# Where the low half of an operand split is made: 64 subtractions of a fused two-block kernel go from VectorE to GpSimd

## The chip, the cores and the metric

The program runs on one core of one Trainium2 chip. The metric is the device time of one execution, in microseconds (us). The profile and the trace come from one execution, taken by the hardware profiler. The engines are called as the profile calls them: PE is TensorE's matmul (PEld its weight load), DVE is VectorE, ACT is ScalarE, POOL is GpSimd, and SP issues most of the DMAs.

## The reference, cut to what matters

The program computes two blocks on 1024 tokens of width 1024 in fp32. The changed lines touch three places: the gated feed-forward part of the first block, the norm at its end with the scale and shift of the second block's first layer, and the norm after that layer with the scale and shift of the next.

```python
def first_block(...):
    ...
        h = h + merged @ w_out[l]
        z = rmsnorm(h, ffn_norm_g[l])
        u = causal_dwconv(z @ w_up[l], conv_w[l], conv_b[l])
        h = h + (jax.nn.silu(u[..., :D_FF]) * u[..., D_FF:]) @ w_down[l]
    return rmsnorm(h[:, N_META:], final_norm_g)
...
def second_block(...):
    for i in range(DEPTH_2):
        ...
        if i % 2 == 0:
            sh, sc, gt = _adaln(c, ab_w_mod[j], ab_b_mod[j])
            h = x * (1.0 + sc[:, None]) + sh[:, None]
            y = _ab_mixer(h, ...)
            ...
            x = _post_norm(x, y, gt[:, None], ab_ln_g[j], ab_ln_b[j])
        else:
            ...
            h = x * (1.0 + sc[:, None]) + sh[:, None]
            f_in, f_gate, cq, ckv, kr, d_gate = _split_cd(h @ cd_w_in[j])
```

`_post_norm` is a layer norm of `ALPHA * x + gate * y`.

## The kernel before, in words

**Matmuls by splits.** PE multiplies fp32 operands in a shorter format, fp32r. Every operand is therefore kept as two parts in a tile of shape `[128, 2, n]`: a high part, which is the fp32 value copied to fp32r by ACT (line 746), and a low part, which is the value less its high part (line 747, a subtraction on DVE). A product of two such operands takes three matmuls for each slice of 128 rows: high weight by high input, high weight by low input, low weight by high input, in this order (`mm3`, line 87 of the profile). `split_act` makes the two parts of an activation; `split_in` does the same for weights that a DMA has brought, with the copy in line 79 and the subtraction in line 80.

**Order.** The program is written in loops, and a scheduler lays every engine's instructions out in one fixed queue when the program is built. At run time each engine takes its queue in that order and waits at an instruction until its inputs are there. Tiles come from pools: a tile whose buffer still serves an earlier reader waits for that reader.

**Unit (lines 936 to 952).** The token axis is cut in four pieces of 258 or 256 columns. The product with `w_up` is done as a block product with seven multiplications instead of eight, so it needs seven inputs T[0] to T[6] for each pair of token pieces, made from eight tiles `z[0]` to `z[7]` (named h in the rows) by sums and differences. There are two pairs, units 0 and 1. `unit` makes the inputs for k = 0 to 3; `put(i, x)` splits x into T[i]. T[0] and T[1] are the pieces as they are and are made early. T[4] is a piece as it is, and T[2], T[3], T[5] and T[6] are differences and sums, made in place. Unit 0's inputs are made during the product with `w_out` (matmuls of line 87, whose results line 898 adds to the residual), unit 1's at the beginning of the product with `w_up` (matmuls of line 1012 in `ffn_up`).

**First norm (`x1_chunk`).** After the last matmuls of `ffn_down` (line 1066, results added by line 1068) the tokens are treated in three chunks of 384, 384 and 256 columns. Per chunk the squares (ACT, line 1115) are added up on DVE (line 1120) and summed over the partitions by a matmul (line 1123); then for each of eight tiles DVE scales by the norm (line 1136), ACT applies scale and shift (line 1140) into one of four buffers, and `split_act` makes `hx`, the input of the second block's first matmuls.

**Second norm (`done` and `emit`, with `ln_chunk`).** The layer norm after that layer goes by the same chunks. `ln_chunk` subtracts the mean on DVE (line 1196), squares on ACT (line 1198), adds the squares up on DVE (line 1204) and sums them by a matmul (line 1207); `emit` multiplies by the norm (DVE, line 1456), scales and shifts (ACT, line 1462) and splits into `hx2` (`hx<-sqt` in the rows). The results of the layer's own last matmuls are added by line 1472 in between.

**POOL** works little: it issues DMAs of an earlier stage (line 1347) and does some memsets and, in the attention at the end, every other addition of 1024 columns (lines 1734 and 1736, `sa`), beside DVE, which does the rest.

Of the kernel before, what the change touches and what calls it, by code (L numbers as in the profile page):

```python
# [8 lines left out]
F32 = mybir.dt.float32  # L9
# [3 lines left out]
ALU = mybir.AluOpType  # L13
# [28 lines left out]
class Build:  # L42
# [696 lines left out]
                pass  # L739


    def split_act(self, t, lo, hi, src, scale=None):
        nc = self.nc
        h = t[:, 0, lo:hi]
        if scale is None:
            nc.scalar.copy(h, src)  # L746
            nc.vector.tensor_tensor(out=t[:, 1, lo:hi], in0=src, in1=h.bitcast(F32), op=ALU.subtract)
        else:
            nc.scalar.mul(h, src, scale)
            nc.vector.scalar_tensor_tensor(out=t[:, 1, lo:hi], in0=src, scalar=scale, in1=h.bitcast(F32), op0=ALU.mult, op1=ALU.subtract)  # L750
# [184 lines left out]
    def unit(self, z, T, n, ch):  # L935
        v = self.nc.vector
        (l1, h1), (l2, h2) = ch
        for k in range(4):
            a, b = z[k][:, l1:h1], z[k][:, l2:h2]
            c, d = z[4 + k][:, l1:h1], z[4 + k][:, l2:h2]  # L940
            put = lambda i, x: self.split_act(T[i], n * k, n * k + n, x)
            put(0, a)
            put(1, c)
            v.tensor_tensor(out=a, in0=a, in1=b, op=ALU.subtract)
            put(3, a)
            v.tensor_tensor(out=b, in0=d, in1=b, op=ALU.subtract)
            put(4, d)
            v.scalar_tensor_tensor(out=d, in0=a, scalar=-1.0, in1=d, op0=ALU.mult, op1=ALU.subtract)
            put(2, d)
            put(5, b)  # L950
            v.tensor_tensor(out=c, in0=c, in1=d, op=ALU.add)
            put(6, c)
            yield
# [173 lines left out]
    def x1_chunk(self, tp, c, lo, hi, rs):  # L1127
        nc, A = self.nc, self.A
        v = nc.vector
        if c == 0:  # L1130
            self.gf = self.load(self.const, "fin_g")
            self.hx = [self.actA.tile([128, 2, T1], F32R, tag="a", name=self.nm("hx")) for _ in range(8)]
        m = self.mod["ab"]
        for k in range(8):
            x = self.h1[k][:, 2 + lo:2 + hi]
            v.scalar_tensor_tensor(out=x, in0=x, scalar=self.gf[:, k:k + 1], in1=rs, op0=ALU.mult, op1=ALU.mult)
            if "x1" in self.dbg:
                nc.sync.dma_start(self.dbg["x1"][k][:, lo:hi], x)
            t = tp.tile([128, 384], F32, tag="tmp", name=self.nm("hx"), bufs=4)[:, 0:hi - lo]
            nc.scalar.activation(t, x, AF.Identity, scale=m[:, 8 + k, 0:1], bias=m[:, k, 0:1])  # L1140
            self.split_act(self.hx[k], lo, hi, t)


    def mods(self, pool, cp):
# [290 lines left out]
    def ab_x(self):  # L1435
        nc, A = self.nc, self.A
# [3 lines left out]
        with ExitStack() as es:  # L1440
# [8 lines left out]
            def done(c, lo, hi, ps):  # L1449
                n = hi - lo  # L1450
                if c == 0:
                    for k in range(8):
                        self.hx2.append(self.actA.tile([128, 2, T1], F32R, tag="a", name=self.nm("hx2")))

                def emit(k, d, rs):
                    v.tensor_tensor(out=d, in0=d, in1=rs, op=ALU.mult)
                    nc.sync.dma_start(self.resd[k][:, lo:hi], d)
                    t = sqt(k)[:, 0:n]
                    if c == 2 and k % 2:
                        v.tensor_scalar(out=t, in0=d, scalar1=sc[:, 0, k:k + 1], scalar2=sc[:, 1, k:k + 1], op0=ALU.mult, op1=ALU.add)  # L1460
                    else:
                        nc.scalar.activation(t, d, AF.Identity, scale=sc[:, 0, k:k + 1], bias=sc[:, 1, k:k + 1])
                    self.split_act(self.hx2[k], lo, hi, t)
                def sqt(k):
                    if k % 2 == 0:
                        self.sqp = tp.tile([128, 1024], F32, tag=("ap", "sg")[k // 2 % 2], name=self.nm("sqt"))
                    return self.sqp[:, 512 * (k % 2):512 * (k % 2) + 384]
                self.ln_chunk(tp, lambda k: self.rx(k, lo, hi), ps, n, emit, sqt, int(c == 2))
# [520 lines left out]
```

## Time and profile before

| what | value |
| --- | --- |
| three executions, median (lowest to highest) | 3126.2 us (3122.37 to 3130.72) |
| the profiled execution's own time | 3125.37 us |
| its span in the trace | 3123.5 us |
| granted PE clock, mean over the span | 0.987 of full speed |
| PE busy | 3000.8 us, 96% |
| DVE busy | 2023.9 us, 65% |
| ACT busy | 1177.7 us, 38% |
| POOL busy | 93.8 us, 3% |

The span is the part of the execution that the trace covers. The busy time of an engine is the time in which one of its instructions ran; an engine that isn't busy waits for another or has nothing to do. Where PE is busy without a break the stage lasts as long as its matmuls. The granted clock says which share of full speed the chip gave PE.

### The profile page before, as it was taken

What the parts mean: (1) busy time and instruction counts of PE and PEld (TensorE: products, weight loads), DVE (VectorE), ACT (ScalarE), POOL (GpSimd) and SP (SyncE); (2) the same over time, 40 slices, a digit from 0 to 9 for tenths busy, and PEclk for the clock granted to TensorE, in tenths of its full rate; (3) what the DMA queues carried; (4) which work ended last, traced back from release to release, by engine and by line L of the source; (5) the groups of instructions that cost most, each with busy time, mean ns of one, the idle gap of its engine ahead of it and who ended that gap; (6) DMA issues with size and microseconds to landing.
All of it is one profiled execution on the core that took longest, in us unless ns stands there. A gap on an engine that the chain in (4) does not pass through costs nothing.

```text
span 3123.5 us, 47333 instructions
## 1 busy us (share of the span) xinstructions
PE 3000.8 (96%) x19205; PEld 2667.8 (85%) x19205; DVE 2023.9 (65%) x3957; ACT 1177.7 (38%) x1851; POOL 93.8 (3%) x99
## 2 busy tenths in 40 slices
PE   8999989999999999989999999998999899999998
PEld 6999977878999999989999997897888787756567
DVE  6549567777456333588777767765434836588876
ACT  5342543332345321244333323234222526355553
POOL 0000000000120000000000000000000000022200
PEclk9999999999999999999999999999999899999999
DMA  4352454343463143432322355501111223400031
GB/s 152 93 167 89 135 193 139 111 137 109 146 183 108 61 133 111 142 95 101 109 100 104 102 183 202 175 29 36 55 48 43 94 70 102 137 4 8 26 110 55
DMA packets 125971, 327.76 MB, mean 105 GB/s; under 512 B 16974, under 2 KB 49966, under 8 KB 125558
## 3 DMA queue, kind: packets, MB, share of 16 engines
q1 hardware_dynamic: 119240, 304.12, 30.6%
q10 hardware_dynamic: 4464, 16.34, 1.3%
q0 software_dynamic: 2048, 4.26, 0.7%
q8 instruction: 151, 2.47, 0.3%
q14 instruction: 68, 0.56, 0.1%
HBM read 250.60 MB, written 73.39 MB: 104 GB/s over the span
## 4 chain that ended last, share of the span: by engine, by line
PE 83%; DVE 9%; ACT 4%; DMA 3%; issue 1%; SPq 0%; ACTq 0%; DVEq 0%
PE mm L87 46%; PE mm L1012 7%; PE sm L1012 7%; PE mm L1066 4%; PE sm L1066 4%; PE mm L1730 3%; PE mm L1284 2%; PE sm L1718 2%; PE sm L1694 1%; DMA YBd<-o 1%; DMA wm<-ab_w_mod 1%; ACT Tt L507 1%; PE sm L1167 1%; PE sm L470 1%; DVE R L609 1%
## 5 line engine op out<-in xcount | busy, mean ns | idle before, releaser
L87 PE MATMUL mm<-z,whl 128*128 128x256 f32 (+3 forms) x4032 | 682.2, 325 | 2.9 <-ACT whl L79 1.5
L87 PEld LDWEIGHTS mm<-z,whl 128*128 128x128 f32 x4032 | 638.5, 190 | 35.9 <-issue 27.4
L80 DVE TENSOR_TENSOR whl<-wraw,whl 128x1024 fp32r<-128x1024 f32 (+2 forms) x200 | 232.9, 1166 | 212.1 <-ACT whl L79 211.7
L87 PE MATMUL mm<-hx,whl 128*128 128x512 f32 (+2 forms) x1608 | 359.5, 381 | 5.6 <-ACT hx L746 4.7
L87 PEld LDWEIGHTS mm<-hx,whl 128*128 128x128 f32 x1608 | 291.3, 189 | 62.6 <-ACT hx L746 5.4
L79 ACT CAST whl<-wraw 128x1024 fp32r<-128x1024 f32 (+2 forms) x200 | 200.2, 1003 | 219.9 <-PE mm L87 135.7
L1012 PE MATMUL sm<-a,whl 128*128 128x256 f32 x1584 | 214.9, 284 | 2.9 <-ACT a L746 1.7
L1012 PE MATMUL mm<-b,whl 128*128 128x258 f32 x1584 | 212.7, 284 | 0.0
L1012 PEld LDWEIGHTS sm<-a,whl 128*128 128x128 f32 x1584 | 201.1, 190 | 5.2 <-ACT a L746 2.4
L1012 PEld LDWEIGHTS mm<-b,whl 128*128 128x128 f32 x1584 | 199.8, 190 | 0.0
L87 PE MATMUL mm<-a,whl 128*128 128x258 f32 (+3 forms) x1344 | 185.2, 300 | 3.7 <-DVE whl L80 3.1
L87 PEld LDWEIGHTS mm<-a,whl 128*128 128x128 f32 x1344 | 184.0, 190 | 4.3 <-DVE whl L80 3.3
L87 PE MATMUL mm<-b,whl 128*128 128x384 f32 (+1 forms) x1152 | 181.6, 319 | 0.0
L87 PEld LDWEIGHTS mm<-b,whl 128*128 128x128 f32 x1152 | 181.4, 188 | 0.0
L87 PE MATMUL mm<-y,whl 128*128 128x256 f32 (+2 forms) x687 | 126.0, 342 | 5.9 <-DVE h L1472 4.1
L87 PEld LDWEIGHTS mm<-y,whl 128*128 128x128 f32 x687 | 110.4, 192 | 20.0 <-DVE h L1472 4.9
L1066 PE MATMUL mm<-g,g 128*128 128x512 f32 (+2 forms) x504 | 116.8, 377 | 4.0 <-ACT g L746 3.9
L1730 PE MATMUL mm<-m,KB 97*128 97x512 f32 x420 | 116.9, 398 | 1.3 <-ACT P L1731 1.3
L1066 PE MATMUL sm<-g,g 128*128 128x512 f32 (+2 forms) x504 | 116.9, 379 | 0.0
L1731 ACT ACTIVATE P<-mm 128x512 f32<-128x512 f32 x160 | 91.6, 596 | 66.0 <-PE mm L1730 48.3
L1695 DVE TENSOR_REDUCE mx<-sm 128x1 f32<-128x512 f32 (+1 forms) x192 | 103.8, 594 | 14.9 <-PE sm L1694 14.1
L1066 PEld LDWEIGHTS mm<-g,g 128*128 128x128 f32 x504 | 91.3, 190 | 21.7 <-ACT g L746 4.8
(586 smaller groups left out, 4656.1 us busy)
## 6 DMA issues: line engine op xcount, KB each, us to landing
wraw<-w_up SPq DMA_DIRECT2D x44, 512.0 KB, 3.8
wraw<-w_h SPq DMA_DIRECT2D x32, 512.0 KB, 3.8
wraw<-ab_w SPq DMA_DIRECT2D x32, 512.0 KB, 4.7
wm<-ab_w_mod SPq DMA_DIRECT2D x24, 512.0 KB
wm<-cd_w_mod SPq DMA_DIRECT2D x24, 512.0 KB, 4.6
gd<-ag SPq DMA_DIRECT2D x22, 512.0 KB, 2.9
av<-gd SPq DMA_DIRECT2D x22, 512.0 KB, 4.7
wd<-w_down SPq DMA_DIRECT2D x22, 512.0 KB
```

The lines of the kernel that those rows point to most:

```text
L79: self.nc.scalar.copy(t[:, 0], raw)
L80: self.nc.vector.tensor_tensor(out=t[:, 1], in0=raw, in1=t[:, 0].bitcast(F32), op=ALU.subtract)
L87: nc.tensor.matmul(ps, W[:, wp, wofs + 128 * k:wofs + 128 * k + 128], X(xp, kofs + k, lo, hi), start=first and k == 0 and i == 0, stop=las ...
L470: nc.tensor.matmul(pw[64 * g2:64 * g2 + 64, NC5 * r:NC5 * r + NC5], Bm[:, q, r, 64 * g2:64 * g2 + 64], ut[:, 2 * q + g2, :], start=True, s ...
L507: (v.tensor_copy if i == 0 and r == g2 else nc.scalar.copy)(Tt.rearrange("p (q g) c -> p g q c", g=2)[R, g2], S[P, 0:NC5, r, 4 * i:4 * i + ...
L1012: nc.tensor.matmul(ps, w[:, wp, o + 128 * k:o + 128 * k + 128], T[i][:, xp, n * k:n * k + n], start=k == 0 and q == 0, stop=k == 3 and q == 2)
L1066: nc.tensor.matmul(ps, w[:, wp, 128 * o:128 * o + 128], g[:, xp, lo:hi], start=n_ == 0 and i == 0, stop=n_ == len(ws) - 1 and i == 2)
L1284: nc.tensor.matmul(ps, X(xp, k, 128 * t, 128 * t + 128), wv[k // 4][:, wp, 256 * (k % 4):256 * (k % 4) + 256], start=k == 0 and i == 0, st ...
L1695: v.tensor_reduce(out=mx[:, qt, j:j + 1], in_=ps, axis=mybir.AxisListType.X, op=ALU.max)
L1718: mm = nc.tensor.matmul(po[64 * c:64 * c + 64, :], vv(t)[:, 64 * h:64 * h + 64], P[t][:, c], start=t == 0, stop=t == KT - 1)
L1730: nc.tensor.matmul(ps, K[0:97, kp, 128 * t:128 * t + 128], Q[0:97, qp, 512 * c:512 * c + 512], start=i == 0, stop=i == 2)
L1731: E[t] = nc.scalar.activation(Pt[:, c], ps, AF.Exp, scale=scale)
```

## The change

`split_act` gets a further argument, the engine that makes the low part. Where it is given, the subtraction is issued on POOL (`nc.gpsimd`) instead of DVE; its operands and its result are the same. It is given for the inputs T[2], T[3], T[5] and T[6] of both units (32 subtractions of 256 or 258 columns), and for the first two chunks of `hx` and of `hx2` (16 each, of 384 columns). After the change every line number beyond 742 is higher by one.

```diff
-    def split_act(self, t, lo, hi, src, scale=None):
+
+    def split_act(self, t, lo, hi, src, scale=None, low=None):
         nc = self.nc
         h = t[:, 0, lo:hi]
         if scale is None:
             nc.scalar.copy(h, src)
-            nc.vector.tensor_tensor(out=t[:, 1, lo:hi], in0=src, in1=h.bitcast(F32), op=ALU.subtract)
+            (low or nc.vector).tensor_tensor(out=t[:, 1, lo:hi], in0=src, in1=h.bitcast(F32), op=ALU.subtract)
...
-            put = lambda i, x: self.split_act(T[i], n * k, n * k + n, x)
+            put = lambda i, x: self.split_act(T[i], n * k, n * k + n, x, low=self.nc.gpsimd if i in (2, 3, 5, 6) else None)
...
-            self.split_act(self.hx[k], lo, hi, t)
+            self.split_act(self.hx[k], lo, hi, t, low=nc.gpsimd if c < 2 else None)
...
-                    self.split_act(self.hx2[k], lo, hi, t)
+                    self.split_act(self.hx2[k], lo, hi, t, low=nc.gpsimd if c < 2 else None)
```

The scheduler lays the queues anew. DVE in unit 0, ahead of the weight split `whl_13308` (line 80) for which PE waits: b_13058, b_13059, b_13061 and b_13062 are T[2], T[3], T[5] and T[6], b_13060 is T[4], and the h tiles are the pieces z. Before:

```order
L898 SCALAR_TENSOR_TENSOR h_1472_12583<-mm_13147,h_1472_12583 128x256
L948 SCALAR_TENSOR_TENSOR h_1500_12851<-h_1472_12583,h_1500_12851 128x258
L747 TENSOR_TENSOR b_13061<-h_1472_12583,b_13061 128x258
L903 TENSOR_TENSOR sqacc<-sqacc,sqt_13174 128x256
L747 TENSOR_TENSOR b_13058<-h_1500_12851,b_13058 128x258
L951 TENSOR_TENSOR h_1500_12851<-h_1500_12851 128x258
L944 TENSOR_TENSOR h_1479_12650<-h_1479_12650 128x258
L747 TENSOR_TENSOR b_13060<-h_1509_12923,b_13060 128x258
L747 TENSOR_TENSOR b_13062<-h_1500_12851,b_13062 128x258
L747 TENSOR_TENSOR b_13059<-h_1479_12650,b_13059 128x258
L946 TENSOR_TENSOR h_1479_12650<-h_1509_12923,h_1479_12650 128x258
L80 TENSOR_TENSOR whl_13308<-wraw_13309,whl_13308 128x1024
```

And after, the same stretch of DVE's queue:

```order
L949 SCALAR_TENSOR_TENSOR h_1500_12851<-h_1472_12583,h_1500_12851 128x258
L945 TENSOR_TENSOR h_1479_12650<-h_1479_12650 128x258
L899 SCALAR_TENSOR_TENSOR h_1472_12583<-mm_13147,h_1472_12583 128x256
L952 TENSOR_TENSOR h_1500_12851<-h_1500_12851 128x258
L947 TENSOR_TENSOR h_1479_12650<-h_1509_12923,h_1479_12650 128x258
L748 TENSOR_TENSOR b_13060<-h_1509_12923,b_13060 128x258
L904 TENSOR_TENSOR sqacc<-sqacc,sqt_13174 128x256
L949 SCALAR_TENSOR_TENSOR h_1509_12923<-h_1479_12650,h_1509_12923 128x258
L80 TENSOR_TENSOR whl_13308<-wraw_13309,whl_13308 128x1024
```

Only the low parts of T[4] (and of T[0] and T[1], earlier) are left on DVE, the sums and differences follow each other directly, and the weight split comes eight rows earlier in the queue (17 rows instead of 25 lie between the unit's first difference, line 944, and it).

POOL's queue in unit 1 (a_13695, a_13696, a_13698 and a_13699 are its T[2], T[3], T[5] and T[6]), the last twelve of 16 rows, in the queue right behind the 16 of unit 0 and ahead of those of `hx`. Before the change POOL's queue has nothing here: the DMAs of line 1347 are followed by the memsets of the attention.

```order
L748 TENSOR_TENSOR a_13698<-h_1467_12520,a_13698 128x256
L748 TENSOR_TENSOR a_13699<-h_1493_12784,a_13699 128x256
L748 TENSOR_TENSOR a_13695<-h_1500_12851,a_13695 128x256
L748 TENSOR_TENSOR a_13698<-h_1472_12583,a_13698 128x256
L748 TENSOR_TENSOR a_13699<-h_1500_12851,a_13699 128x256
L748 TENSOR_TENSOR a_13698<-h_1479_12650,a_13698 128x256
L748 TENSOR_TENSOR a_13696<-h_1486_12717,a_13696 128x256
L748 TENSOR_TENSOR a_13695<-h_1509_12923,a_13695 128x256
L748 TENSOR_TENSOR a_13698<-h_1486_12717,a_13698 128x256
L748 TENSOR_TENSOR a_13699<-h_1509_12923,a_13699 128x256
L748 TENSOR_TENSOR a_13695<-h_1512_12955,a_13695 128x256
L748 TENSOR_TENSOR a_13699<-h_1512_12955,a_13699 128x256
```

All sixteen stand in one queue, and the last but one is T[2]'s for k = 3.

DVE in the second norm, from chunk 0's products with the norm (h tiles, line 1456) to the first additions of chunk 1's squares (line 1204). Before, from the fifth product on:

```order
L1456 TENSOR_TENSOR h_2146_18884<-h_2146_18884,rsy_23019 128x384
L747 TENSOR_TENSOR hx_2634_22980<-sqt_23028,hx_2634_22980 128x384
L747 TENSOR_TENSOR hx_2635_22981<-sqt_23028,hx_2635_22981 128x384
L1456 TENSOR_TENSOR h_2147_18886<-h_2147_18886,rsy_23019 128x384
L1456 TENSOR_TENSOR h_2148_18888<-h_2148_18888,rsy_23019 128x384
L1456 TENSOR_TENSOR h_2149_18890<-h_2149_18890,rsy_23019 128x384
L747 TENSOR_TENSOR hx_2636_22982<-sqt_23039,hx_2636_22982 128x384
L747 TENSOR_TENSOR hx_2637_22983<-sqt_23039,hx_2637_22983 128x384
L1192 TENSOR_SCALAR mu_23162<-sm_23160 128x384
L1472 SCALAR_TENSOR_TENSOR h_2144_18880<-mm_23244,mod_ab,h_2144_18880 128x256
L747 TENSOR_TENSOR hx_2638_22984<-sqt_23050,hx_2638_22984 128x384
L747 TENSOR_TENSOR hx_2639_22985<-sqt_23050,hx_2639_22985 128x384
```

And after, from the fifth product on:

```order
L1457 TENSOR_TENSOR h_2146_18884<-h_2146_18884,rsy_23019 128x384
L1457 TENSOR_TENSOR h_2147_18886<-h_2147_18886,rsy_23019 128x384
L1457 TENSOR_TENSOR h_2148_18888<-h_2148_18888,rsy_23019 128x384
L1457 TENSOR_TENSOR h_2149_18890<-h_2149_18890,rsy_23019 128x384
L1193 TENSOR_SCALAR mu_23162<-sm_23160 128x384
L1473 SCALAR_TENSOR_TENSOR h_2144_18880<-mm_23244,mod_ab,h_2144_18880 128x256
L1197 TENSOR_TENSOR h_2142_18876<-h_2142_18876,mu_23162 128x384
L1197 TENSOR_TENSOR h_2143_18878<-h_2143_18878,mu_23162 128x384
L1197 TENSOR_TENSOR h_2144_18880<-h_2144_18880,mu_23162 128x384
L1197 TENSOR_TENSOR h_2145_18882<-h_2145_18882,mu_23162 128x384
```

The eight low parts have left this queue, and chunk 1's differences from the mean (line 1196, now 1197) follow the products directly. The squares of chunk 1 (ACT) write buffers that chunk 0's `sqt` tiles used, and so wait for POOL's subtractions from these.

## Rows read from the trace of the kernel before

**Rows 1.** The page, part 1: busy us, share of span, instructions.

```profile
PE 3000.8 (96%) x19205; PEld 2667.8 (85%) x19205; DVE 2023.9 (65%) x3957; ACT 1177.7 (38%) x1851; POOL 93.8 (3%) x99
```

**Rows 2.** Busy time by window: window, its length, each engine's busy us, clock, DMA.

```profile
1340.00:1370.00 30.00, 24.57 (x188) 23.91 (x188) 28.91 (x75) 14.77 (x36) 0.00 (x0) 0.94 0.25 77
1400.00:1422.00 22.00, 17.59 (x103) 15.30 (x104) 20.05 (x55) 10.02 (x26) 0.00 (x0) 0.84 0.08 28
2109.00:2136.00 27.00, 18.84 (x93) 16.76 (x92) 18.52 (x43) 17.35 (x40) 0.00 (x0) 0.81 0.07 21
2446.00:2493.00 47.00, 32.78 (x172) 28.68 (x171) 43.95 (x101) 32.05 (x68) 0.00 (x0) 0.82 0.37 123
```

**Rows 3.** Timeline, unit 0: start, length, engine, line, operation [idle before <- releaser].

```profile
1350.68 0.76 DVE L944 TENSOR_TENSOR h<-h 128x258 f32<-128x258 f32 x2
...
1359.11 1.22 DVE L80 TENSOR_TENSOR whl<-wraw,whl 128x1024 fp32r<-128x1024 f32 x1
...
1360.38 4.36 PE L87 MATMUL mm<-a,whl 128*128 128x256 f32 x22 [3.12 <-DVE whl L80]
...
1365.33 4.89 PE L87 MATMUL mm<-a,whl 128*128 128x254 f32 x39 [0.59 <-DVE h L898]
```

**Rows 4.** Chain of waits, window 1400 to 1422: total us, times, longest.

```profile
PE sm L1012 <- ACT a L746: 1.7, 3, 0.6
...
PE sm L1012 <- DVE a L747: 1.2, 3, 0.5
```

**Rows 5.** Timeline, unit 1.

```profile
1396.86 2.79 DVE L747 TENSOR_TENSOR a<-h,a 128x256 fp32r<-128x256 f32 x8
...
1408.25 0.76 DVE L944 TENSOR_TENSOR h<-h 128x256 f32<-128x256 f32 x2
...
1420.25 0.43 DVE L747 TENSOR_TENSOR a<-h,a 128x256 fp32r<-128x256 f32 x1
```

**Rows 6.** Timeline, first norm, end of chunk 1.

```profile
2121.59 1.22 PE L1123 MATMUL sm<-cse,ones 128*128 128x256 f32 x2 [2.30 <-DVE cse L1120]
```

**Rows 7.** Timeline, second norm, chunks 0 and 1.

```profile
2462.61 1.62 PE L1207 MATMUL sm<-sqt,ones 128*128 128x384 f32 x2 [6.39 <-DVE sqt L1204]
...
2468.89 7.00 PE L87 MATMUL mm<-hx,whl 128*128 128x384 f32 x38
...
2472.22 1.03 DVE L747 TENSOR_TENSOR hx<-sqt,hx 128x384 fp32r<-128x384 f32 x2
...
2478.58 1.02 DVE L747 TENSOR_TENSOR hx<-sqt,hx 128x384 fp32r<-128x384 f32 x2
```

**Rows 8.** Line 747 by form: count, ns min/median/max, first and last start.

```profile
L747 DVE TENSOR_TENSOR hx<-hx,hx x24: 415/552/560, 2091.9 to 2136.5; 128x384 fp32r<-128x384 f32 x16, 128x256 fp32r<-128x256 f32 x8
```

**Rows 9.** POOL: the attention's additions by tile, and a memset by line.

```profile
L1736 POOL TENSOR_TENSOR sa<-sa,P x12: 2370/2382/2990, 2759.6 to 2948.7; 128x1024 f32<-128x1024 f32 x12
...
L1980 POOL MEMSET const-float32-0.0<- 128x1 f32 x1 | 0.1, 104 | 0.2 <-issue 0.2
```

**Rows 10.** Timeline, three places in the attention where POOL works.

```profile
2759.61 2.37 POOL L1736 TENSOR_TENSOR sa<-sa,P 128x1024 f32<-128x1024 f32 x1 [10.20 <-ACT P L1731]
2760.14 2.39 DVE L1685 TENSOR_TENSOR qt<-qt,qu 32x512 f32<-32x512 f32 x1
...
2788.03 3.47 POOL L1734 TENSOR_TENSOR sa<-P,P 128x1024 f32<-128x1024 f32 x1 [18.15 <-ACT P L1731]
2788.10 1.16 DVE L1734 TENSOR_TENSOR sa<-P,P 128x1024 f32<-128x1024 f32 x1
2789.18 2.87 DVE L1752 TENSOR_TENSOR gt<-gt,rz 128x512 f32<-128x512 f32 x1
...
2826.66 2.38 POOL L1734 TENSOR_TENSOR sa<-P,P 128x1024 f32<-128x1024 f32 x1 [14.23 <-ACT P L1731]
2827.64 0.35 DVE L1666 TENSOR_TENSOR kt<-kt,mm 64x256 f32<-64x256 f32 x1
```

**Rows 11.** Line 1685, all its instructions: ns min/median/max.

```profile
L1685 DVE TENSOR_TENSOR qt<-qt,qu x16: 675/683/2389, 2695.9 to 2943.9; 32x512 f32<-32x512 f32 x16
```

## The prediction

> **What bounds the kernel now.** I read the page's busy table first: TensorE is busy for 96% of the span, DVE for 65%, POOL for 3% [rows 1]. So a microsecond counts only where TensorE stands still, and DVE is not the bound over the whole. Next I cut the span at the places where the 64 moved subtractions lie, with the table of busy time by window [rows 2]. There the picture is another one: in the stretch that makes unit 0's inputs DVE works 28.9 of 30 us, in unit 1's 20.1 of 22, in the second chunk of the first norm 18.5 of 27, in the second norm 44.0 of 47, and TensorE leaves 4 to 14 us of each idle, at a granted clock of 0.81 to 0.94. These are the few places where DVE sets the pace. Then I read the timeline of each to see which DVE instruction releases TensorE:
>
> - Unit 0: TensorE stands 3.12 us until the weight split `whl` of line 80, which starts at 1359.11, and 22 matmuls later 0.59 us for line 898 [rows 3]. Line 80 stands in DVE's queue behind all of the unit's work.
> - Unit 1: from 1411 on the matmuls of `ffn_up` eat the products' inputs as fast as they are made; TensorE waits 1.7 us in all for high parts and 1.2 us for low parts [rows 4]; the low part that starts at 1420.25 is the last but one [rows 5].
> - First norm, chunk 1: TensorE waits 2.30 us for the sum of squares of chunk 2, whose six additions stand on DVE behind the last low parts of chunk 1 [rows 6].
> - Second norm: TensorE waits 6.39 us for the sum of squares of chunk 1, which stands on DVE behind all eight low parts of chunk 0; then it works on matmuls of `hx`, chunk 0 [rows 7].
>
> **What is moved.** 64 subtractions leave DVE for POOL: 32 of 256 or 258 columns (0.43 us each [rows 5]) and 32 of 384 columns (0.55 us each [rows 8]). One after the other they cost DVE less, since neighbours overlap: eight of 256 columns take 2.79 us, so 0.336 each (2.79 less the 0.08 by which the last overhangs, over 8) [rows 5]; two of 384 take 1.03, so 0.47 each [rows 7]. DVE is relieved of 32 x 0.336 + 32 x 0.47 = 25.8 us. The copies on ACT stay, the DMAs of SP too.
>
> **What one costs on POOL.** The trace has no subtraction of this size there. The nearest rows are the attention's additions of 1024 columns, 2.37 to 2.38 us where nothing disturbs them, and a memset of one column, 0.104 us [rows 9]. A straight line through the two gives 0.68 us for 256 columns and 0.96 for 384. Bounds: purely proportional, 0.59 and 0.89; with another 0.25 us for each instruction, which no row excludes, 0.93 and 1.21. I take the line. A move thus doubles the time of each subtraction, which would be no harm if POOL worked beside DVE.
>
> **Whether it works beside DVE.** The attention stage shows that it does not. At 2759.61 POOL starts an addition; the DVE addition of line 1685, both inputs in SBUF, comes at 2760.14 and takes 2.39 us instead of its usual 0.68: it ends 0.55 us after POOL is through [rows 10, 11]. The other way round, a POOL addition that comes at 2788.03, together with one of DVE at 2788.10, takes 3.47 us, and DVE's next (512 columns) takes 2.87: POOL waited for DVE, took its turn between two DVE instructions, and DVE waited for it whole. A DVE addition with one input in PSUM, at 2827.64, takes 0.35 us in the middle of a POOL addition and waits for nothing [rows 10]. So POOL and those DVE instructions that read two tensors in SBUF take turns, one whole instruction each. The Trainium skill says the same ("SBUF — State Buffer", section "Who interferes with whom"): a DVE instruction with two SBUF inputs contends with a POOL instruction that reads SBUF, because its second input comes through the read port that the two engines share. By that rule the sum comes out as by the rows, and the trace agrees with it, at 2.39 against 0.68 us. This counts against the change: around the moved subtractions nearly all of DVE's work reads two SBUF tensors (lines 80, 797, 912, 944 to 951, 1120, 1136, 1196, 1204, 1456, and the low parts that remain). Only lines 898, 1068, 1192, 1472 and the evacuations of `ffn_up` read PSUM. What was 0.336 or 0.47 us on DVE becomes 0.68 or 0.96 us of the same shared resource.
>
> **The sum, place by place.** I lay POOL's and DVE's instructions in their new order end to end and let only the PSUM readers run beside POOL. The same arithmetic has to give the times of before: in unit 0, 25 rows from 1350.68 to line 80 at 0.336 make 8.4 us, so 1359.08, and the row says 1359.11 [rows 3]; in unit 1, 34 rows and a weight split of half the width (half of line 80's 1.22) from 1408.25 make 12.0 us, so 1420.28, and the row says 1420.25 [rows 5].
>
> 1. Unit 0. Ahead of line 80 there are now 17 DVE rows (two of PSUM) and nine or ten POOL subtractions that are ready by then: 17 x 0.336 + 9.5 x 0.68 = 12.2 us, less 0.3 to 0.7 beside PSUM readers: 1362.4 instead of 1359.1, and TensorE begins some 3.4 us later. After that, ahead of line 898, come line 80 itself, six DVE rows and the other six POOL ones, 1.2 + 2.0 + 4.1 us: TensorE's next matmuls, at 1365.33 now, could begin at 1370.1, 4.8 later, of which 3.4 are counted. **+5** (3.5 with the lower POOL prices, or if line 898 delays nothing).
> 2. Unit 1. Eight of DVE's 28 low parts are made long before, 16 go. Of the 34 rows 20 stay; with the weight split and 14 POOL subtractions they stand ahead of the last but one: 6.7 + 0.6 + 9.5 = 16.8 us from 1408.25, so it starts at 1425.1 and ends at 1425.8, where it ends at 1420.7 now. TensorE has nothing but these products then. **+5** (4 to 5.5).
> 3. First norm. In chunk 0 DVE has no gap; its queue holds line 1068, which frees TensorE's PSUM, so the chunk's eight POOL instructions cost about 0.7 us at the sum of squares. In chunk 1 eight of 0.96 replace eight of 0.47, +3.9; DVE idles 8.5 us of that stretch [rows 2], and I let its gaps take up near half: sum of squares +2.1. **+2.8** (1.5 to 4).
> 4. Second norm. Chunk 0: +3.9 in the same way, and ACT's squares of chunk 1 use the buffers that POOL's last subtractions still read, two more turns of 0.96: the sum of squares comes some 6 us later (2468.6 against 2462.6). In chunk 1 the low parts run from 2472.2 to 2479.6; eight of 0.96 and the eleven or so DVE rows of 0.47 between them take 12.9 us, to 2485, and what is left of chunk 0's delay comes on top, so about 2487, and the squares of chunk 2 with them. But here TensorE has other work, matmuls of `hx` that need chunk 0 alone (38 of them take 7.0 us [rows 7]), and fills later waits with it. Of two delays of 6 to 7 us I count a quarter, what those matmuls don't fill. **+3** (1 to 6, the worst known term).
>
> Sum 5 + 5 + 2.8 + 3 = +15.8 on the profiled execution's 3125.4 us: **3141 us**. That execution lies 0.8 under the median of three (3126.2), so the two may be taken as one. Nothing else should move: in POOL's queue its other work stands ahead of and behind these places, and SP's order is as before.
>
> **The rivals.**
>
> - *Relief*: short instructions interleave after all, POOL really works beside DVE. The rows above, with 0.68-us victims, speak against it. It would bring: line 80 earlier by eight rows, 2.6 us; unit 1 bound by 15 POOL subtractions from 1409, 1419.4 instead of 1420.7, so 1.3; the first norm 0.5; the second 3 to 4 of its 6.39. Together -8: 3117. It decides if a DVE subtraction beside a POOL one keeps its 0.43 us.
> - *Small delay*: they take turns, but the matmuls in hand swallow the norms' delays and POOL costs the lower price: 3.5 + 4 + 1 = +8.5, 3134; hardly to be measured.
> - *Dearer*: each POOL instruction costs 0.25 us more. Behind some 15 in each unit that is 3.8 us twice, about 2 in each norm, so near +27: 3153. For it speaks that a short instruction shows a fixed cost that 1024 columns hide; against it, that the memset of one column, which also pays such a cost, takes 0.104 us [rows 9].
>
> The page "GPSIMD Engine Reference" of the Trainium skill (section 3.1, "Elementwise — side-by-side cycle accounting") has 4497 ns for 2048 columns; a line through that and the 2.38 us here gives, as an estimate, 0.79 and 1.05 us, and the sum would be near +20; no run here shows it.
>
> **How the numbers follow.** Chances: as summed 0.55 (its own range 3135 to 3147), small delay 0.24, dearer 0.12, relief 0.09. Faster or slower by 0.3% is 9.4 us, about what can be told from no change. Relief at -8 lies just inside, but may bring more than I count: 0.06 of its 0.09 as faster. Same: the small delay, the rest of relief, and the lower edge of the main case: 0.29. Slower 0.65. The range from 3122 to 3154 leaves out relief and the end of dearer.
>
> **What would show it.** In the changed profile: POOL L748 at 0.7 us (256 columns) and 1.0 (384) or longer where it waits its turn; DVE's subtractions and scalings beside it at 0.7 to 1.4 instead of 0.43; TensorE's wait for line 80 in unit 0 at 6 to 7 us instead of 3.12, its waits for low parts in unit 1 at 6 instead of 1.2 and now for POOL; the waits for sums of squares longer. It is wrong if DVE's neighbours keep their 0.43, or if POOL's durations are far from 0.68 and 0.96.

## The result and the profile after

| | median (lowest to highest), us | executions |
| --- | --- | --- |
| before | 3127.06 (3120.29 to 3130.72) | 6 |
| after | 3144.58 (3140.29 to 3150.31) | 6 |

The ratio is 1.006, 95% interval 1.0044 to 1.0075: the change makes the kernel 14 to 23 us slower. The profiled execution took 3144.98 us with a span of 3143.2 us, 19.7 us more than before, at a clock of 0.984.

On the page, part 1 answers to [rows 1]; below it are two rows of part 5.

```profile
PE 3009.4 (96%) x19205; PEld 2673.0 (85%) x19205; DVE 2015.5 (64%) x3893; ACT 1177.5 (37%) x1851; POOL 168.2 (5%) x163
...
L87 PE MATMUL mm<-hx,whl 128*128 128x512 f32 (+2 forms) x1608 | 366.2, 384 | 22.0 <-ACT fx L1542 7.6
...
L1013 PE MATMUL sm<-a,whl 128*128 128x256 f32 x1584 | 213.3, 284 | 7.8 <-POOL a L748 6.3
```

DVE has lost 64 instructions but only 8.4 us of busy time, where 25.8 us of work were taken from it; POOL has gained 74.4. An instruction that waits for its turn counts as busy, and that is where the rest of DVE's relief is: measured against the median of the same form before, DVE's rows at the changed places are 16.8 us longer in all. Of TensorE's new idle time two releasers stand out: POOL in the product with `w_up`, 6.3 us, and an evacuation on ACT, `fx` (its copy of a finished product `mm`), 7.6 us, which the prediction did not name.

POOL's subtractions by form: count, ns min/median/max, first and last start.

```profile
L748 POOL TENSOR_TENSOR b<-h,b x16: 641/843/1620, 1353.2 to 1368.4; 128x258 fp32r<-128x258 f32 x16
L748 POOL TENSOR_TENSOR a<-h,a x16: 715/728/5761, 1412.0 to 1428.2; 128x256 fp32r<-128x256 f32 x16
L748 POOL TENSOR_TENSOR hx<-hx,hx x16: 1017/1154/1346, 2096.9 to 2124.9; 128x384 fp32r<-128x384 f32 x16
L748 POOL TENSOR_TENSOR hx<-sqt,hx x16: 1003/1183/5082, 2454.5 to 2491.3; 128x384 fp32r<-128x384 f32 x16
```

Undisturbed, 256 columns take 0.72 us and 384 take 1.00; the maxima of 5.76 and 5.08 us are waits, not work.

To see where the time went, PE's matmuls were counted in order of their starts, and the span between the starts of the same two matmuls was taken in both traces. Over all the runs below the early stages vary by up to 8 us and the three places by up to 2 where nothing was changed in them, so only larger differences mean something. Units 0 and 1 are added, since the cut between them shifts.

```
matmuls, by number in PE's order      before   after
to 9000, early stages                 1301.2   +1.5
9000 to 9800, units 0 and 1            120.9   +3.9
9800 to 14300, ffn_up, ffn_down        654.2   -0.2
14300 to 14700, first norm              78.3   +0.3
14700 to 16150, second block's layer   277.5    0.0
16150 to 16400, second norm             60.8  +11.1
16400 to the end                       614.8   +2.9
```

The timeline after, at the four places (start, length, engine, line, operation [idle before <- releaser]); it answers to [rows 3], [rows 5], [rows 6] and [rows 7]. Here and below only the rows that the text uses are shown; others lie between them.

```profile
1352.21 0.76 DVE L945 TENSOR_TENSOR h<-h 128x258 f32<-128x258 f32 x2
...
1355.96 10.01 POOL L748 TENSOR_TENSOR b<-h,b 128x258 fp32r<-128x258 f32 x11 [1.25 <-ACT b L747]
1357.84 0.97 DVE L947 TENSOR_TENSOR h<-h,h 128x258 f32<-128x258 f32 x1
1358.74 0.95 DVE L748 TENSOR_TENSOR b<-h,b 128x258 fp32r<-128x258 f32 x1
1361.27 1.75 DVE L80 TENSOR_TENSOR whl<-wraw,whl 128x1024 fp32r<-128x1024 f32 x1
1363.07 11.15 PE L87 MATMUL mm<-a,whl 128*128 128x256 f32 x69 [4.30 <-DVE whl L80]
...
1411.10 0.75 DVE L945 TENSOR_TENSOR h<-h 128x256 f32<-128x256 f32 x2
1412.04 16.89 POOL L748 TENSOR_TENSOR a<-h,a 128x256 fp32r<-128x256 f32 x16 [42.97 <-ACT a L747]
1416.81 0.41 DVE L748 TENSOR_TENSOR a<-h,a 128x256 fp32r<-128x256 f32 x1
1417.85 0.58 PE L1013 MATMUL sm<-a,whl 128*128 128x256 f32 x1 [3.00 <-POOL a L748]
...
2110.18 0.91 PE L1124 MATMUL sm<-cse,ones 128*128 128x384 f32 x2 [1.13 <-DVE cse L1121]
...
2128.56 0.70 PE L1124 MATMUL sm<-cse,ones 128*128 128x256 f32 x2 [1.78 <-DVE cse L1121]
...
2474.69 8.78 PE L87 MATMUL mm<-hx,whl 128*128 128x384 f32 x47
...
2491.86 0.63 PE L820 MATMUL sm<-sqt,ones 128*32 128x256 f32 x4
...
2497.53 0.59 PE L815 MATMUL sm<-sqt,ones 128*128 128x256 f32 x2
2497.78 1.90 PE L87 MATMUL mm<-hx,whl 128*128 128x384 f32 x9
...
2506.72 0.47 ACT L1542 COPY fx<-mm 128x384 f32<-128x384 f32 x1
2507.24 7.95 PE L87 MATMUL mm<-hx,whl 128*128 128x384 f32 x30 [7.56 <-ACT fx L1542]
```

The end of the second norm before, in the same view; these rows the prediction did not use.

```profile
2479.04 2.90 PE L819 MATMUL sm<-sqt,ones 128*32 128x256 f32 x14 [3.15 <-ACT sqt L1198]
...
2483.38 0.60 PE L814 MATMUL sm<-sqt,ones 128*128 128x256 f32 x2
2483.63 8.75 PE L87 MATMUL mm<-hx,whl 128*128 128x384 f32 x48
...
2492.58 0.47 ACT L1541 COPY fx<-mm 128x384 f32<-128x384 f32 x1
...
2493.10 12.11 PE L87 MATMUL mm<-hx,whl 128*128 128x384 f32 x77 [0.73 <-ACT fx L1541]
```

This is the difference that matters most. Before, the sums of squares of chunk 2 (line 819, last sum line 814) stand in PE's queue ahead of 48 matmuls of `hx` (the third weight panel on chunk 0 and the first on chunk 1), whose inputs are ready. From the start of the last sum to ACT's evacuation `fx`, which comes in ACT's queue behind the scalings and copies of chunk 2 and starts at 2492.58, there are 9.2 us, and the 48 matmuls cover them: TensorE waits 0.73 us. After, the scheduler has set most of these 48 among and ahead of the sums. At the last sum (line 815, 2497.53) nine are left, 1.90 us; the way to `fx` is as long as before (2506.72, again 9.2 us after), and TensorE stands 7.56 us.

The chain of waits of after, in unit 1 (window 1398 to 1430) and in the second norm (2450 to 2512): total us, times, longest.

```profile
PE sm L1013 <- POOL a L748: 6.3, 6, 3.0
...
PE sm L909 <- DVE sqacc L904: 2.5, 1, 2.5
...
PE sm L1013 <- ACT a L747: 1.5, 1, 1.5
...
ACT sqt L1199 <- POOL hx L748: 8.6, 7, 1.6
...
PE mm L87 <- ACT fx L1542: 7.6, 1, 7.6
```

### The profile page after: what moved, and what is told of

Its sections match the earlier page's. It is cut to its first block, busy times and chain, and to the rows that moved or that the text cites. A ratio compares the mean times of both kernels' runs of the same rounds, so it can differ in the third digit from the quotient of the medians.

```text
span 3143.2 us, 47400 instructions
## 1 busy us (share of the span) xinstructions
PE 3009.4 (96%) x19205; PEld 2673.0 (85%) x19205; DVE 2015.5 (64%) x3893; ACT 1177.5 (37%) x1851; POOL 168.2 (5%) x163
## 4 chain that ended last, share of the span: by engine, by line
PE 81%; DVE 9%; ACT 4%; DMA 3%; issue 1%; POOL 1%; SPq 0%; ACTq 0%; DVEq 0%; POOLq 0%
PE mm L87 45%; PE mm L1013 7%; PE sm L1013 7%; PE sm L1067 4%; PE mm L1067 4%; PE mm L1731 3%; PE sm L1719 2%; PE mm L1285 2%; DMA YBd<-o 1%; PE sm L1695 1%; ACT Tt L507 1%; DVE R L609 1%; PE sm L470 1%; ACT whl L79 1%; DMA wm<-ab_w_mod 1%
## 5 line engine op out<-in xcount | busy, mean ns | idle before, releaser
L87 PE MATMUL mm<-hx,whl 128*128 128x512 f32 (+2 forms) x1608 | 366.2, 384 | 22.0 <-ACT fx L1542 7.6
```

Source lines behind the costliest of these rows:

```text
L87: nc.tensor.matmul(ps, W[:, wp, wofs + 128 * k:wofs + 128 * k + 128], X(xp, kofs + k, lo, hi), start=first and k == 0 and i == 0, stop=las ...
```

## The experiments

Diffs are against the changed kernel unless the text says before. "Stages" are the surplus over the kernel before in units 0 and 1 / first norm / second norm, by the count of matmuls above; after itself has +3.9 / +0.3 / +11.1.

### One part alone

Three kernels give POOL one place each: the units (e1), the first norm (e2), the second norm (e3). As an example e1:

```diff
-            self.split_act(self.hx[k], lo, hi, t, low=nc.gpsimd if c < 2 else None)
+            self.split_act(self.hx[k], lo, hi, t)
...
-                    self.split_act(self.hx2[k], lo, hi, t, low=nc.gpsimd if c < 2 else None)
+                    self.split_act(self.hx2[k], lo, hi, t)
```

> Only the 32 low parts of the units are made by POOL; both norms as before. By the terms of the prediction +10 us (3136): +5 in unit 0, +5 in unit 1. By the trace of the changed kernel, where TensorE is 1.2 us late at the weight split of unit 0 but waits no longer for line 898 (0.59 before), and 3.5 us later after unit 1, +4 us (3130): a POOL subtraction beside DVE costs turns in unit 0, but DVE has given up 8 of 25 rows in exchange. Rival: all of it is fluctuation of the earlier stages and the units cost nothing, within 1 us of before.

> Only the 16 low parts of the first norm's chunks 0 and 1 are made by POOL. By the prediction's term +2.8 us (3129). By the trace of the changed kernel, in which TensorE is 5.4 us behind ahead of this stage and 5.7 behind it, +0.3 to +1 us: the matmuls in hand cover chunk 0 and the gaps of DVE take up chunk 1.

> Only the 16 low parts of the second norm's chunks 0 and 1 are made by POOL. By the prediction's term +3 us (3129): matmuls of hx in hand fill most of the two delays. By the trace of the changed kernel +11 us (3137): POOL's first subtraction of chunk 0 and of chunk 1 waits 4 to 5 us behind DVE instructions that follow each other without a pause, ACT's squares wait for POOL, ACT's weight copy and evacuations stand behind these, and so TensorE runs out of matmuls all the same (waits of 6.4 and 7.6 us). If the second is right, e1, e2 and e3 add up to about the 17 us of the whole change, with e3 more than half.

| run | ratio to before (95%) | worked out, us | stages |
| --- | --- | --- | --- |
| e1, units | 1.0018 (1.0009 to 1.0027) | +5.6 | +3.8 / +0.3 / 0.0 |
| e2, first norm | 1.0007 (0.9999 to 1.0016) | +2.2 | +0.3 / +2.2 / -0.5 |
| e3, second norm | 1.0045 (1.0029 to 1.0061) | +14.0 | -0.1 / +1.7 / +12.0 |

The microseconds are the ratio less 1 by the 3120.15 us of before on that chip. Their sum, 21.8, agrees with the whole within its interval. The second norm, forecast at +3, makes up most of it; the units cost about half of the +10 forecast. The first norm's cost lies between nothing and 2 us: e3, which changes nothing there, shows +1.7 as well.

### Low parts left out

POOL's subtraction becomes a memset to zero. The kernel leaves out the low parts of those 64 operands, so its time is that of a kernel in which neither DVE nor POOL makes them.

```diff
-            (low or nc.vector).tensor_tensor(out=t[:, 1, lo:hi], in0=src, in1=h.bitcast(F32), op=ALU.subtract)
+            if low:
+                low.memset(t[:, 1, lo:hi].bitcast(F32), 0.0)
+            else:
+                nc.vector.tensor_tensor(out=t[:, 1, lo:hi], in0=src, in1=h.bitcast(F32), op=ALU.subtract)
```

> The 64 POOL instructions only write zeros (a memset of the low part) and read nothing; so the low parts of these inputs are left out of the products. DVE is relieved of the same 64 subtractions. If the loss comes from POOL's subtractions (their reads of SBUF, their length, their turns), this must be faster than before: by the relief worked out in the prediction -8 us (3118), with DVE's neighbours at 0.42 us. If the loss comes from what else the change does (the new order of the queues, waits on POOL as such), it stays slower than before, above +5.

It took 3108.1 us, ratio 0.9962 (0.9948 to 0.9975), -11.9 us; stages -11.3 / -0.9 / +2.1. By form and from the timeline:

```profile
L749 POOL MEMSET hx<- x32: 417/418/425, 2044.7 to 2385.0; 128x384 f32 x32
...
L749 POOL MEMSET b<- x16: 303/304/314, 1284.3 to 1288.2; 128x258 f32 x16
```

```profile
2465.09 1.92 PE L87 MATMUL mm<-hx,whl 128*128 128x384 f32 x9
...
2474.62 5.58 PE L87 MATMUL mm<-hx,whl 128*128 128x384 f32 x22 [7.61 <-ACT fx L1545]
```

The memsets need no input and ran far ahead of their places (unit 0's by 1288.2), so this run does not show a POOL instruction working beside DVE's chains. DVE's and ACT's orders are those of after, and PE's differs in six places. What it shows is the worth of the relief: the units do gain 11 us when nobody makes these low parts, and TensorE never waits for them. So the loss is not that DVE's relief is worthless there, nor the new order of DVE; it is what the subtractions cost on POOL. In the second norm, where DVE is relieved of 16 instructions and POOL disturbs nobody, the stage is not shorter than before: TensorE still stands 7.61 us for `fx`. But PE's order there is that of after, with nine matmuls left at the last sum, so this run does not say that the relief is worthless in the second norm; what it gains may be hidden by the order (e11 below, an order like it with all low parts made, has +5.1, which is 3.0 more).

### Two of four inputs

Only T[5] and T[6] of the units go to POOL, 16 subtractions; both norms stay on DVE.

```diff
-            put = lambda i, x: self.split_act(T[i], n * k, n * k + n, x, low=self.nc.gpsimd if i in (2, 3, 5, 6) else None)
+            put = lambda i, x: self.split_act(T[i], n * k, n * k + n, x, low=self.nc.gpsimd if i in (5, 6) else None)
```

> Only T[5] and T[6] of both units on POOL (16 subtractions), both norms as before. TensorE needs these two last in unit 1, so POOL may be late with them while DVE gets to T[2] and T[3] 2.7 us earlier (8 x 0.336). If POOL's turns (0.59 us each beside DVE) and its lateness are the whole price: unit 0 about +1, unit 1 -1 to -2.5, within 2 us of before. If any subtraction on POOL costs the same wherever it is needed: half of the +4 us that the trace of the changed kernel shows for both units.

3123.06 us, ratio 1.0007 (0.9994 to 1.002); units +2.0. No gain that the measurement can see, and no loss: half the subtractions, and about half the surplus of e1 in the units.

### Each subtraction twice

e1, with every subtraction of the units done twice on POOL.

```diff
             (low or nc.vector).tensor_tensor(out=t[:, 1, lo:hi], in0=src, in1=h.bitcast(F32), op=ALU.subtract)
+            if low:
+                low.tensor_tensor(out=t[:, 1, lo:hi], in0=src, in1=h.bitcast(F32), op=ALU.subtract)
```

> As e1 (the units alone on POOL), but each POOL subtraction is made twice. If the price is POOL's turns and its own length: ahead of unit 0's weight split some 9 more turns of 0.59 us, +5; unit 1 has 15 more of 0.68 us ahead of the low part that TensorE needs, +10; so some 15 us above e1, 3140. If POOL's work were hidden, the time of e1.

3142.91 us, ratio 1.0075 (1.0056 to 1.0093); units +20.2, so 16.4 above e1. In the chain of waits of unit 1 TensorE now stands for POOL alone:

```profile
PE sm L1015 <- POOL a L750: 13.9, 7, 3.8
```

Here, where there is nothing to relieve DVE of, the 32 added instructions cost 0.51 us of TensorE's time each.

### Own buffers for the second norm

In the second norm ACT's squares of the next chunk waited 8.6 us for buffers that POOL's subtractions still read. e6 gives four of the eight `sqt` tiles of `emit` in chunks 0 and 1 a buffer of their own; e7 does the same to the kernel before.

```diff
-                    t = sqt(k)[:, 0:n]
+                    if c < 2 and k == 0:
+                        self.tq = yp.tile([128, 2, 1024], F32R, tag="y", name=self.nm("tq")).rearrange("p a b -> p (a b)").bitcast(F32)
+                    t = self.tq[:, 512 * k - 2048:512 * k - 2048 + n] if c < 2 and k > 3 else sqt(k)[:, 0:n]
```

> The changed kernel, but in the second norm the last four of eight scaled tiles of chunks 0 and 1 lie in a buffer of their own, so that the first four of ACT's squares of the next chunk find free buffers and the others wait for POOL's first four subtractions instead of its last. If ACT's squares waiting for POOL (8.6 us in all in the changed kernel's second norm) are what makes this stage late, its surplus over before falls from 11 us to 4 to 7, and the time to about 3139 against 3144. If POOL's late low parts themselves are what TensorE waits for, the stage stays at +11.

> The kernel before with the same buffers as e6 and all low parts on DVE: a control. Nothing waited for these buffers for long there, so the time is that of before within 2 us; if it gets faster by more, the gain of e6 is not to be put down to POOL.

e6: 3140.6 us, ratio 1.0067 (1.0047 to 1.0087), second norm +11.2, as without the buffers. e7: 1.0003 (0.9992 to 1.0013). From e6's chain of waits, and its timeline:

```profile
ACT sqt L1199 <- POOL hx L748: 0.6, 1, 0.6
```

```profile
2487.98 6.46 PE L87 MATMUL mm<-hx,whl 128*128 128x384 f32 x27 [2.09 <-POOL hx L748]
2494.37 0.62 PE L820 MATMUL sm<-sqt,ones 128*32 128x256 f32 x4
...
2509.74 5.49 PE L87 MATMUL mm<-hx,whl 128*128 128x384 f32 x16 [7.55 <-ACT fx L1544]
```

The wait was taken away, 0.6 us of 8.6 are left, and nothing was won. The sums of squares now start at 2494.37 directly behind 27 matmuls of `hx` in PE's queue: the order hides the gain. So the theory that the buffers alone were the cause fell, and PE's order had to be tried.

### PE's order in the second norm

e9 is e6 with one more rule for the scheduler: the third panel of `hx`, chunk 0, may stand only behind the last sum of squares of chunk 2, as it does before. e10 is after with the same rule, without the buffers.

```diff
-                self.panels(((w, ev), self.kv_panel(tp, 0), self.gate_panel(tp, 0, "gx", 1)), X, 8, CHX)
+                self.panels(((w, ev), self.kv_panel(tp, 0), self.gate_panel(tp, 0, "gx", 1)), X, 8, CHX, after=self.tailmm)
```

Here `tailmm` is that last sum, and `after` adds the rule to the panel's first matmul. e11 goes the other way: the kernel before, all low parts on DVE, with the norm of chunk 2 laid out so that PE's sums stand among the panels much as in after. In the traces e10 differs from after, and e9 from e6, in PE's order alone (36 places); e11 differs from before in 29 places of PE's order and also in about a dozen rows each of DVE's and ACT's.

```diff
-                self.ln_chunk(tp, lambda k: self.rx(k, lo, hi), ps, n, emit, sqt, int(c == 2))
+                with (self.tc.high_priority() if c == 2 else ExitStack()):
+                    self.ln_chunk(tp, lambda k: self.rx(k, lo, hi), ps, n, emit, sqt, int(c == 2))
```

> e6 with one ordering added on TensorE: the third panel of hx matmuls (chunk 0) and the fourth (chunk 1) come behind the sums of squares of chunk 2, as in the kernel before; in e6 and in the changed kernel these sums are interleaved with the end of the two panels, whose matmuls wait for POOL's low parts of chunk 1. If this order is what holds the last chunk back, the sums follow ACT's squares directly (squares end at 2491.7 in e6, the last sum at 2500.0), the two panels cover the chain after it again (TensorE's wait of 7.6 us for the evacuation goes below 2), and the stage's surplus falls from 11 to about 5 us: 3135 against e6's 3141. If POOL's low parts as such set the end, nothing is gained: 3141.

> The changed kernel itself with the same ordering as e9 and its own buffers. ACT's squares of chunk 2 still wait for POOL here (the last ends at 2493.1, the last sum at 2497.5), so the order alone gives back only some 2 us of the stage's 11: about 3142. If order alone is the cause it gives back as much as e9, 6 us; if the buffers alone mattered, e6 would have shown it.

> The kernel before, all low parts on DVE, but the scheduler is made to lay the sums of squares of chunk 2 among the third and fourth panel, as in the changed kernel (the layer norm's last chunk has another priority). If the order as such costs, its second norm is 3 to 7 us longer and TensorE waits for the evacuation there as in the changed kernel: 3125 to 3129 against 3120. If it costs only together with POOL's late low parts, the time of before within 2 us.

| run | buffers | PE's order | low parts | ratio (95%) | second norm |
| --- | --- | --- | --- | --- | --- |
| e11 | old | like after | DVE | 1.0025 (1.0015 to 1.0035) | +5.1 |
| e10 | old | like before | POOL | 1.0047 (1.0033 to 1.0061) | +6.9 |
| e6 | own | like after | POOL | 1.0067 (1.0047 to 1.0087) | +11.2 |
| e9 | own | like before | POOL | 1.0042 (1.0029 to 1.0054) | +2.3 |

The timelines of e11, e10 and e9 at the last sum and the wait for `fx`:

```profile
2480.76 0.59 PE L814 MATMUL sm<-sqt,ones 128*128 128x256 f32 x2
2481.00 2.97 PE L87 MATMUL mm<-hx,whl 128*128 128x384 f32 x15
2490.41 9.92 PE L87 MATMUL mm<-hx,whl 128*128 128x384 f32 x45 [6.43 <-ACT fx L1542]
```

```profile
2482.38 1.37 PE L823 MATMUL sm<-sqt,ones 128*32 128x256 f32 x4 [3.79 <-ACT sqt L1202]
...
2490.89 9.21 PE L87 MATMUL mm<-hx,whl 128*128 128x384 f32 x48
2500.58 1.66 PE L87 MATMUL mm<-hx,whl 128*128 128x384 f32 x8 [0.47 <-ACT fx L1545]
```

```profile
2481.30 2.89 PE L823 MATMUL sm<-sqt,ones 128*32 128x256 f32 x14 [3.75 <-ACT sqt L1202]
...
2485.43 8.75 PE L87 MATMUL mm<-hx,whl 128*128 128x384 f32 x48
2494.90 7.26 PE L87 MATMUL mm<-hx,whl 128*128 128x384 f32 x40 [0.73 <-ACT fx L1547]
```

e11, without one instruction on POOL, costs 5.1 us in that stretch and 7.8 us (4.7 to 10.9) in the time: the wait for `fx` is back, 6.43 us. Since rows of DVE and ACT moved with it, this is not PE's order by itself; e10 and e9 show that. PE's order restored gives 4.2 of after's 11.1 back with the old buffers, and 8.9 of e6's 11.2 with the own buffers; the wait falls to 0.47 and 0.73. The buffers give 4.6 more once the order is right, and nothing while it is not. What both leave, 2.3, is more than the -0.5 to +0.2 of the kernels that change nothing in the second norm (e1, e2, e5, e8, e12); its cause stays open. All four kernels are still slower than before.

### Only what is ready early

Only T[0] and T[1] of unit 1, whose eight low parts DVE makes at 1396.86 [rows 5], go to POOL.

```diff
-            put = lambda i, x: self.split_act(T[i], n * k, n * k + n, x, low=self.nc.gpsimd if i in (2, 3, 5, 6) else None)
+            put = lambda i, x: self.split_act(T[i], n * k, n * k + n, x, low=self.nc.gpsimd if i < 2 and l1 else None)
```

(Both norms stay on DVE.)

> Only the first two inputs of the second unit (8 subtractions of 256 columns) go to POOL; their high parts are cast 4 us before DVE's splits of that unit begin, so POOL can be through before DVE's chain starts. Theory (POOL costs only where its subtractions meet DVE's unbroken chain): DVE loses 8 times 0.336, 2.7 us, ahead of the sums for which PE waits 4.0 us, so the stretch of the two units is 1 to 3 us shorter than in the kernel before, and the time lies within 0.1% of it. Rival (every low part given to POOL costs about 0.15 us net, as in the whole set): 0 to 3 us longer. The time alone can hardly tell these apart; PE's stretch of the second unit is read beside it.

3120.12 us, ratio 0.9999 (0.9988 to 1.0011); units +0.8, unit 1 +0.2. The time is within what the theory gave, but the 1 to 3 us are not there. From the timeline:

```profile
1392.34 7.14 POOL L748 TENSOR_TENSOR a<-h,a 128x256 fp32r<-128x256 f32 x8 [466.91 <-ACT a L747]
1395.38 1.26 DVE L982 TENSOR_TENSOR whl<-wsum,whl 128x1024 fp32r<-128x1024 f32 x1 [2.13 <-ACT whl L981]
1396.57 0.94 DVE L904 TENSOR_TENSOR sqacc<-sqacc,sqt 128x254 f32<-128x254 f32 x1
1397.57 0.74 PE L909 MATMUL sm<-sqacc,ones 128*128 128x254 f32 x2 [4.11 <-DVE sqacc L904]
```

DVE was freed of its 2.8 us and then stood 2.13 us for ACT's copy of a weight, and the sum for which TensorE waits took a turn behind POOL, 0.94 instead of 0.42 us. TensorE waits 4.11 us, before 4.00:

```profile
1401.49 1.22 PE L908 MATMUL sm<-sqacc,ones 128*128 128x254 f32 x2 [4.00 <-DVE sqacc L903]
```

Another engine was next in line, so the relief was worth nothing at this place.

## Why the prediction was right in its total and wrong in two terms

The forecast of 3141 and the finding that POOL and DVE share a resource held; of the rivals, *relief* (-8), *small delay* (+8.5) and *dearer* (+27) lie outside the measured 14 to 23 us. But two terms missed in opposite directions: 10 forecast for the units and 3.9 measured, 3 for the second norm and 11.1 measured. That the total is nearer than its parts is luck: 6.1 too much and 8.1 too little nearly cancel.

**POOL's price.** The straight line gave 0.68 and 0.96 us; undisturbed, the last three of unit 1 together last 2.11 us with 0.73 for the last one, so they start 0.69 us apart; those of 384 columns last 1.00 to 1.02 at least. Right; *dearer* is out.

```profile
1426.82 2.11 POOL L748 TENSOR_TENSOR a<-h,a 128x256 fp32r<-128x256 f32 x3
```

**Taking turns.** DVE's rows in unit 0 last 0.95 and 0.97 us instead of 0.43 [rows 5], as forecast: longer by 0.52 to 0.54, most of one turn of the other engine (0.69). In unit 1 it went otherwise, see below. The page "SBUF — State Buffer" of the Trainium skill (section "Who interferes with whom") has the same rule for two SBUF inputs against POOL's reads, and the rows of unit 0 agree.

**Unit 0, forecast +5.** The step that was mis-sized is the price of a pair. I added a DVE row and a POOL row, 0.336 + 0.68 = 1.02 us; in the alternating stretch the two DVE rows above start 0.90 us apart with one POOL row between them. Over the whole stretch a POOL row cost still less: from the unit's first difference (1352.21) to line 80 (1361.27) DVE's 17 rows take 9.1 us, forecast 11.7, before 8.4 for 25; with the 0.53 us by which line 80 itself is longer, the nine POOL rows that start ahead of it cost DVE 0.43 us each on top of its own 0.336 a row, where 0.68 were counted. Some DVE rows had no POOL row beside them (POOL stood 1.25 us for a copy of ACT). The wait for line 80 grew from 3.12 to 4.30, not to 6 or 7, and the 0.59 us for line 898 are gone: TensorE's waits there grew by 0.6 us.

**Unit 1, forecast +5.** The step on the path was right: from the start of the first difference (1411.10) to that of the last but one low part (1427.51, 0.69 before the last) there are 16.4 us, forecast 16.8, before 12.0. But it came about in another way than told: POOL at first did not take turns, it stood 5.76 us behind DVE's chain and then ran nearly alone. DVE's neighbours kept their 0.41 us there, which the prediction had named as a sign of being wrong; yet POOL's wait made the sum the same. TensorE's waits for high and low parts rose from 2.9 to 7.8 us [rows 4], nearly the 5 forecast; its wait for the sum of line 904 fell from 4.00 (line 903 before) to 2.5, which I had not counted, and that for the sum before it grew from 2.83 to 3.14. Both units together: 0.6 + 0.3 + 4.9 - 1.5 = 4.3 us, and the count of matmuls has 3.9; behind these waits the granted clock fell towards the lower of its two levels (1.2 GHz) in other places, to a mean of 0.57 from 1403 to 1405 before and of 0.59 from 1394 to 1397 after, so the two need not agree more closely.

**First norm, forecast +2.8.** Between nothing and 2 us. The wait for the sum of squares of chunk 2 was 2.30 [rows 6] and is 1.78; that for chunk 1's, which had none, is 1.13. The runs cannot place the cost closer.

**Second norm, forecast +3.** Here a step failed, not only a size: "here TensorE has other work, matmuls of `hx` that need chunk 0 alone [...], and fills later waits with it", so that I counted a quarter of the delays. This took PE's queue as unchanged. The scheduler lays every queue anew, and had put those matmuls ahead of the sums of chunk 2; they no longer stood where they cover the chain to `fx`. I had looked at the rows of DVE and POOL and not at PE's. By the count of matmuls TensorE has lost 1.9 us in this stretch up to matmul 16370, just ahead of the wait for `fx`, and 11.1 up to 16390, just behind it. The runs put 4.2 us on that order with the old buffers (e10 against after), 8.9 with the new (e9 against e6), and 4.6 on ACT's squares that wait for POOL's reads once the order is right (e9 against e10). The two hide each other: each remedy alone brought at most 4.2 us, both together 8.8. That ACT's squares use buffers POOL still reads had been named, at two turns of 0.96 us; the row says 8.6 us, in seven waits.

**What DVE's relief was worth.** I had taken the second norm as a place where DVE sets the pace, 44 of 47 us [rows 2], and gave *relief* 3 to 4 us there. e4 takes the work away entirely and is not shorter there, since `fx` is late as in after; as PE's order is that of after too, no run shows what the relief is worth in the second norm under the order of before. In the units it is worth 11.3 us with nobody making these low parts, where *relief*, with POOL making them, counted 3.9. But POOL's subtractions cost more than the relief brings, and no kernel that computes everything came out faster than before.

Still open: the 2.3 us that e9 leaves in the second norm; the 2.9 us of after in the last stretch, which in the kernels that leave the second norm alone is between -0.5 and +4.2; and the 5.5 us by which e9's time (+13.1, interval 9.0 to 16.9) exceeds its three stages (3.0 + 2.3 + 2.3), of which 2.8 lie in the last stretch.

## What to carry to other kernels

When an instruction goes to another engine and a scheduler lays the queues, compare the queue of the bound engine, not only those of the two engines named in the change: here 4.2 of the 11.1 us of the largest term came back when PE's matmuls alone were put back in place, and 8.9 of 11.2 where the buffers had been parted too. Before work is moved to a spare engine, ask whether the two share something; the price can then be as much as the slower engine's time on the same resource, and the busy table does not show it. When one wait is taken away and the time stays, try the next in line together with it before the first is called innocent.

## What the hardware showed that was not expected

The two engines do not always take turns. In unit 0 they alternate, one instruction each. In unit 1 POOL's first subtraction starts at 1412.04 and lasts 5.76 us, through some fifteen DVE instructions that follow each other without a gap and none of which is longer than before (0.41 us). It ends about 0.6 us after the last of them (1416.81 + 0.41).

```profile
1412.04 5.76 POOL L748 TENSOR_TENSOR a<-h,a 128x256 fp32r<-128x256 f32 x1 [42.97 <-ACT a L747]
```

In the second norm two take 4.99 and 5.08 us in the same way. So, as far as these three rows go, an unbroken chain of DVE instructions with two SBUF inputs can keep POOL out for the whole of it; that the chain is the cause is read from the times and was not tried by a run. The section of the Trainium skill named above says that the issue order decides who blocks; by that one would expect POOL's instruction to go ahead of the later of those fifteen, and these rows differ. In unit 0 POOL did get in between neighbouring DVE instructions (0.97 and 0.95 us above), and in the first norm none of its sixteen took more than 1.35 us; what decides between the two cases was not found.
